# Making less of the last S5 layer in advance: V and the taps move back into the layer, powers, rotation and W stay ahead of it

## The chip, the cores and the metric

The kernel runs on one core of one Trainium2 chip. The metric is the device time of one execution in microseconds (us), and the median of several runs is compared. Engines are named as the profile names them: PE is TensorE (matmuls and transposes), PEld its weight loads, DVE is VectorE, ACT is ScalarE, POOL is GpSimd, and SP is SyncE, which here only issues DMAs. ACT issues a few DMAs too.

## The reference, cut to what matters

The program is a trunk of four layers over 512 tokens of width 1024, in float32. Layer 0 is an S5 mixer, layer 1 an HGRN2 mixer, layer 2 sliding-window attention, and layer 3 an S5 mixer again with its own weights.

```python
for i in range(4):
    u = rms_norm(h, norm_pre[i])
    y = (s5_branch, hgrn2_branch, swa_branch)[i % 3](u, ...)
    h = h + rms_norm(y, norm_post[i])

# s5_branch: 64 groups of 16 channels, 64 complex states each
proj = h @ w_in; u, z = split(proj)
a = exp(lambda * dt)                 # complex, one per group and state
b = (a - 1) / lambda * B             # complex input matrix
x_t = a * x_{t-1} + b @ u_t          # scan over the 512 tokens
y = gelu(2 * Re(C @ x) + d * u)
y = y * sigmoid(y @ w_glu + b_glu)
return (y * silu(z)) @ w_out
```

What an S5 layer needs besides its activations depends on its parameters alone: the powers a^0 to a^8, the input matrix over a chunk of eight tokens (V), the output matrix over a chunk (W), the direct response inside a chunk (the taps, which fill a Toeplitz matrix), and a rotation table for the scan over 64 chunks. None of it depends on the tokens, so it can be made at any time before the layer.

## The kernel before, in words

**Layers.** Every layer begins with the transposed normalised input (`norm_xt`, L279: eight transposes for a 128-token block, each evacuated twice, as a rounded high part `xh` on ACT and a remainder `xl` on DVE). Big projections are done as three matmul terms, high by high, high by low and low by high (`ws_steps`, L220; `as_steps`, L235). Weights come in 512 KB pieces by SP and are split in the same way (`w_conv`, L159: `whi` on ACT, `wlo` on DVE). Every layer ends with `out_proj` (L328), whose matmuls are named `ops` and which adds the result to the residual `h` (L350), a tile of 16 KB a partition, and spills `h` to DRAM (`hd`, L356).

**The S5 layer** (`layer_s5`, L1026). The 64 groups are handled as eight blocks b of eight groups. For a block, `s5_u` (L837) evacuates a projection to `ut`, writes it to DRAM (`ub`) and reads it back with the chunks spread over partitions (`u`). `s5_core` (L854) multiplies V by u (`xps`), rotates, scans (`r`, L879), rotates back into `spre`, and adds two products, Toeplitz by u and W by states (`yps`, L902 and L904). The result goes through gelu and two transposes a pair of blocks to `y`. `s5_rest` (L928) is the input projection itself, 16 blocks of PE work of which the first four are done in halves of 256 tokens. After it `s5_yparts` (L983) splits `y` into `yh` and `yl`, and `s5_glu_first` (L997) begins the gate's projection.

In layer 0 the constants are made inside the layer: `s5_tables` (powers), `s5_v` (V, L747), `s5_taps` (L779: 8 small matmuls `kps`, 8 transposes `tps`, 2 transposes `ktp`, and 8 DMAs that fill the Toeplitz matrix `toep`), `s5_rot` and `s5_w`. In layer 3 `s5_load` (L652) loads all of it from DRAM: V, rotation, taps (as 8 DMAs a block straight into `toep`) and W.

The order inside an S5 layer is written out: each part is a Python generator that yields (engine, cost, marks it needs), and `Flow` (L58) picks again and again the step that can start first by those planned costs. The queues of PE, DVE, ACT and SP follow that order. A DMA is planned with 4.5 us to landing, a block's eight `toep` DMAs with 0.6 us of the DMA queue.

**What is made ahead** (before). `ahead_plan` (L625) makes a list of jobs for layer 3: one `ahead_base` (powers and tables), four `ahead_rot`, and eight `ahead_block` (L557), each of which makes V, the taps and W of one block and writes them to DRAM. A job is a generator too. The HGRN layer calls `ahead(1)` at 88 places (L1299, L1306), the attention layer `ahead(3)` after each of its 22 steps (L1486). Base and rotation take 40 calls, a block takes 12, so HGRN has room for four blocks, and attention makes the other four. The jobs' tiles lie where `h` lies: both layers release `h` first (`close_h`) and load it again from `hd` behind the jobs (`open_h`, L1514).

In these two layers the order is not written out by hand: the framework's scheduler places the instructions by its own estimates. Buffers are handed out in program order, though. The jobs' `kps`, `tps` and `ktp` take PSUM buffers of the tag `ca`, of which there are two, and the HGRN core (`dps`, `sps`, `bps`, `cps`), the attention scores (`scps`, L1364) and the input transposes (`xtp`) take theirs from the same two.

**Attention** (`layer_at`, L1417) runs the steps of `ATSEQ` (L48): c is the softmax of a pair of heads over one 128-token block (`at_core`, L1346), g a gate (`at_gate`), q and z projections. The last steps are c12, z3, c13 and four gates.

Of the kernel before, what the change touches and what calls it, by code (L numbers as in the profile page):

```python
# [108 lines left out]
class Trunk:  # L109
# [447 lines left out]
    def ahead_block(self, j, b):  # L557
        nc, a = self.nc, self.a
        gs = slice(8 * b, 8 * b + 8)
        shp = [P, 8, 8, 16]  # L560
        with self.tc.tile_pool(name="ahead", bufs=1, reuse_waits="tile") as s:
            prm = s.tile([P, 4, 128], F32, tag="prm", name="prm")
            nc.sync.dma_start(out=prm, in_=a["s5_bc"][j, b])
            ap = s.tile([P, 2, 8, 9], F32, tag="ap", name="aps")
            nc.sync.dma_start(out=ap, in_=self.sd["ap"][:, :, gs, :])
            co = s.tile([P, 2, 2, 8], F32, tag="co", name="cos")
            nc.sync.dma_start(out=co, in_=self.sd["co"][:, :, :, gs])
            dm = s.tile([P, 8], F32, tag="dm", name="dms")
            nc.gpsimd.memset(dm, 0.0)
            nc.sync.dma_start(out=dm[0:16, :], in_=a["s5_d"][j][:, gs])  # L570
            c1 = s.tile([P, 8, 32], F32, tag="c1", name="c1")
            nc.gpsimd.memset(c1[:, :, 16:32], 0.0)
            yield
            B = prm.rearrange("p k (g h) -> p k g h", h=16)
            q = s.tile([P, 2, 8, 16], F32, tag="q12", name="q12")
            q2 = s.tile([P, 2, 8, 16], F32, tag="q12b", name="q12b")
            nc.vector.tensor_tensor(out=q, in0=B[:, 0:2], in1=bc(co[:, 0].unsqueeze(3), [P, 2, 8, 16]), op=ALU.mult)
            nc.vector.tensor_tensor(out=q2, in0=B[:, 0:2][:, ::-1], in1=bc(co[:, 1].unsqueeze(3), [P, 2, 8, 16]), op=ALU.mult)
            nc.vector.tensor_tensor(out=q, in0=q, in1=q2, op=ALU.add)
            nc.scalar.activation(out=c1[:, :, 0:16], in_=B[:, 2], func=AF.Copy, scale=self.cst[:, CO_SGN:CO_SGN + 1])  # L580
# [5 lines left out]
            nc.vector.tensor_tensor(out=t2, in0=bc(ap[:, 1, :, 0:8].unsqueeze(3), shp), in1=bc(q[:, 1].unsqueeze(2), shp), op=ALU.mult)
            yield
            nc.vector.tensor_tensor(out=vt, in0=vt, in1=t2, op=ALU.add)
            yield
            vtf = vt.rearrange("p g j h -> p g (j h)")  # L590
            kps = self.psum.tile([P, 2, 128], F32, tag="ca", name="kps", bufs=2)
            for g in range(8):
                c = 32 * (g % 4)
                nc.tensor.matmul(kps[c:c + 32, g // 4, :], lhsT=c1[:, g, :], rhs=vtf[:, g, :], start=True, stop=True)
            kt = s.tile([P, 2, 128], F32, tag="q12b", name="kt")
            nc.scalar.activation(out=kt, in_=kps, func=AF.Copy)
            yield
            v = s.tile([P, 8, 128], F32, tag="v", name="v")
            for hh in range(2):
                tps = self.psum.tile([P, 4, 128], F32, tag="ca", name="tps", bufs=2)  # L600
                for g in range(4):
                    nc.tensor.transpose(tps[:, g, :], vtf[:, 4 * hh + g, :], self.ident)
                nc.scalar.activation(out=v[:, 4 * hh:4 * hh + 4, :], in_=tps, func=AF.Copy)
            nc.sync.dma_start(out=self.sd["v", b], in_=v)
            yield
            ktp = self.psum.tile([P, 2, 4, 32], F32, tag="ca", name="ktp", bufs=2)
            for i in range(2):
# [1079 lines left out]
```

## Time and profile before

Three runs of the kernel before took 1133.0, 1134.98 and 1136.96 us; the median is 1134.98 us. The profiled execution took 1136.95 us, of which 1135.1 us lie between its first and last instruction.

| engine | busy us | share of the span | instructions |
|---|---|---|---|
| PE | 1040.9 | 92% | 6480 |
| PEld | 824.9 | 73% | 6480 |
| DVE | 750.9 | 66% | 1466 |
| ACT | 498.1 | 44% | 921 |
| POOL | 93.7 | 8% | 167 |

The span divides about so: layer 0 to 264 us, HGRN to 586, its output projection to 630, attention to 857, its output projection to 886, the S5 part of layer 3 to 1028, the gate to 1090, and the last output projection to the end. Busy time is what an engine spent in instructions. A busy PE need not be at its peak, since matmuls overlap and run at half speed when the granted clock is at its lower level; the column PEclk gives the granted clock as a share of full speed.

### The profile page before, as it was taken

Reading aid. Unit: us, or ns where it says so; the run is one execution under the profiler, and the core shown is the slowest. Engines: PE = TensorE matmul, PEld = TensorE weight load, DVE = VectorE, ACT = ScalarE, POOL = GpSimd, SP = SyncE. Lnnn points to the kernel's source line nnn. Section 1 sums busy time; section 2 is a strip of 40 time slices with the busy share of each in tenths; the row PEclk is TensorE's granted clock in tenths of the full one; section 3 lists DMA queues with packets and bytes.
Section 4 is the critical chain, followed back from the end, with each engine's and each line's share of the span. In section 5 each row is a group of like instructions: output and inputs, shape, how many; then the busy total and the mean of one; then the engine's idle time right before and its main releaser. Section 6 shows DMA issues by size and latency. Waiting matters only on the chain. (4 is left out here: it accounts for less than half of the span.)

```text
span 1135.1 us, 17074 instructions
## 1 busy us (share of the span) xinstructions
PE 1040.9 (92%) x6480; PEld 824.9 (73%) x6480; DVE 750.9 (66%) x1466; ACT 498.1 (44%) x921; POOL 93.7 (8%) x167
## 2 busy tenths in 40 slices
PE   5999976999899999999999899999979989988997
PEld 4755544778899898988968886666637867766876
DVE  6686759585698877687865755877836435643752
ACT  4344426554442324243234424587544436644441
POOL 2000000120200001000001021100000100000200
PEclk9999987999999999999999899999969989998999
DMA  5564233534242313422263254331512567844231
GB/s 226 145 183 129 61 95 89 178 113 153 96 131 92 101 43 122 126 91 74 90 224 112 84 148 111 108 98 64 180 63 94 172 194 230 246 154 148 93 111 56
DMA packets 77185, 142.69 MB, mean 126 GB/s; under 512 B 33584, under 2 KB 44592, under 8 KB 75952
## 3 DMA queue, kind: packets, MB, share of 16 engines
q1 hardware_dynamic: 72128, 126.32, 35.9%
q10 hardware_dynamic: 4976, 15.28, 4.1%
q8 instruction: 51, 0.84, 0.3%
q14 instruction: 30, 0.25, 0.1%
HBM read 107.53 MB, written 24.87 MB: 117 GB/s over the span
## 5 line engine op out<-in xcount | busy, mean ns | idle before, releaser
L183 DVE TENSOR_TENSOR wlo<-wraw,whi 128x1024 fp32r<-128x1024 f32 x116 | 144.9, 1264 | 102.1 <-ACT whi L182 90.9
L228 PE MATMUL pj<-xh,whi 128*128 128x512 f32 (+1 forms) x496 | 180.6, 367 | 1.5 <-ACT rraw L1337 1.5
L228 PE MATMUL pj<-xl,whi 128*128 128x512 f32 (+1 forms) x496 | 177.7, 360 | 0.0
L228 PE MATMUL pj<-xh,wlo 128*128 128x512 f32 (+1 forms) x496 | 176.8, 357 | 0.0
L182 ACT ACTIVATE whi<-wraw 128x1024 fp32r<-128x1024 f32 x116 | 121.0, 1056 | 81.0 <-PE pj L228 41.2
L228 PE MATMUL pj<-xf,wraw 128*128 128x512 f32 (+1 forms) x320 | 116.7, 514 | 0.0
L228 PEld LDWEIGHTS pj<-xh,whi 128*128 128x128 f32 x496 | 96.4, 196 | 16.8 <-issue 4.3
L228 PEld LDWEIGHTS pj<-xl,whi 128*128 128x128 f32 x496 | 96.4, 195 | 14.5 <-issue 3.6
L243 PE MATMUL ops<-whi,gh 128*128 128x512 f32 x256 | 101.6, 399 | 4.5 <-ACT gh L1089 2.2
L228 PEld LDWEIGHTS pj<-xh,wlo 128*128 128x128 f32 x496 | 96.1, 194 | 12.6 <-issue 1.1
L243 PE MATMUL ops<-wlo,gh 128*128 128x512 f32 x256 | 100.7, 394 | 2.6 <-DVE wlo L183 2.6
L243 PE MATMUL ops<-whi,gl 128*128 128x512 f32 x256 | 100.3, 394 | 0.1
L228 PEld LDWEIGHTS pj<-xf,wraw 128*128 128x128 f32 x320 | 59.8, 194 | 40.5 <-issue 36.7
L243 PEld LDWEIGHTS ops<-whi,gh 128*128 128x128 f32 x256 | 48.0, 188 | 16.4 <-ACT gh L1089 3.0
L243 PEld LDWEIGHTS ops<-wlo,gh 128*128 128x128 f32 x256 | 48.1, 188 | 14.9 <-DVE wlo L183 5.1
L243 PEld LDWEIGHTS ops<-whi,gl 128*128 128x128 f32 x256 | 48.1, 188 | 11.7 <-DVE gl L1090 0.9
L228 PE MATMUL pj<-yl,whi 128*128 128x512 f32 x128 | 51.2, 400 | 2.5 <-DVE yl L994 2.5
L228 PE MATMUL pj<-yh,whi 128*128 128x512 f32 x128 | 51.7, 404 | 2.0 <-ACT whi L182 2.0
L228 PE MATMUL pj<-yh,wlo 128*128 128x512 f32 x128 | 51.2, 400 | 1.1 <-DVE wlo L183 1.1
L243 PE MATMUL vps<-wlo,xh 128*128 128x256 f32 x160 | 45.3, 283 | 0.0
L243 PE MATMUL vps<-whi,xl 128*128 128x256 f32 x160 | 45.3, 283 | 0.0
L243 PE MATMUL vps<-whi,xh 128*128 128x256 f32 x160 | 45.3, 283 | 0.0
(296 smaller groups left out, 2075.3 us busy)
## 6 DMA issues: line engine op xcount, KB each, us to landing
wraw<-in_s_in SPq DMA_DIRECT2D x32, 512.0 KB, 5.8
wraw<-in_hg_in SPq DMA_DIRECT2D x32, 512.0 KB, 3.6
wraw<-in_at_in SPq DMA_DIRECT2D x20, 512.0 KB, 4.5
wraw<-in_s_glu SPq DMA_DIRECT2D x16, 512.0 KB, 4.1
wraw<-in_s_out SPq DMA_DIRECT2D x16, 512.0 KB, 3.5
hd<-h SPq DMA_DIRECT2D x6, 1024.0 KB, 4.1
h<-hd ACTq DMA_DIRECT2D x3, 2048.0 KB, 7.9
prm<-in_s_bc SPq DMA_DIRECT2D x16, 256.0 KB, 3.8
```

What stands on the lines that cost most here:

```text
L182: nc.scalar.activation(out=hi, in_=raw, func=AF.Copy)
L183: nc.vector.tensor_tensor(out=lo, in0=raw, in1=hi.bitcast(F32), op=ALU.subtract)
L228: self.nc.tensor.matmul(ps, lhsT=l[k // 4][:, k % 4, c], rhs=r[:, k, n0:n1], start=k == 0 and n == 0, stop=k == KB - 1 and n == len(terms) ...
L243: self.nc.tensor.matmul(ps, lhsT=l[:, k, c], rhs=r[k // per][:, k % per, :], start=k == 0 and n == 0, stop=k == KB - 1 and n == 2)
```

## The change

HGRN makes the base, the rotation and all eight W (`ahead_w`, 6 calls a job, so 48 calls in place of four blocks' 48). V and the taps of layer 3 are made in layer 3 by the functions that layer 0 uses. Layer 3 loads the powers, the coefficients and `d` at its start, and per block the parameters, the rotation and W. The Toeplitz DMAs read from SBUF instead of DRAM. Attention runs no jobs and keeps `h`. Two more edits belong to it: V's and the parameters' tiles lie in the layer's own pool in layer 3, and the first chunk of the gate's weights is converted when input chunk 6 is done (`early`), no longer at the end of the projection.

```diff
-    def ahead_block(self, j, b):
+    def ahead_w(self, j, b):
...
-            prm = s.tile([P, 4, 128], F32, tag="prm", name="prm")
-            nc.sync.dma_start(out=prm, in_=a["s5_bc"][j, b])
-            ap = s.tile([P, 2, 8, 9], F32, tag="ap", name="aps")
+            prm = s.tile([P, 2, 128], F32, tag="prm", name="prm", bufs=2)
+            nc.sync.dma_start(out=prm, in_=self.a["s5_bc"][j, b][:, 2:4])
+            ap = s.tile([P, 2, 8, 9], F32, tag="ap", name="aps", bufs=2)
             nc.sync.dma_start(out=ap, in_=self.sd["ap"][:, :, gs, :])
...
+            c1 = s.tile([P, 8, 16], F32, tag="c1", name="c1", bufs=2)
+            nc.scalar.activation(out=c1, in_=B[:, 0], func=AF.Copy, scale=self.cst[:, CO_SGN:CO_SGN + 1])
             yield
-            vt = s.tile(shp, F32, tag="vt", name="vt")
...
+            w = s.tile(shp, F32, tag="w", name="w", bufs=2)
+            t2 = s.tile(shp, F32, tag="t2", name="t2w")
+            nc.vector.tensor_tensor(out=w, in0=bc(ap[:, 0, :, 1:9].unsqueeze(3), shp), in1=bc(c1.unsqueeze(2), shp), op=ALU.mult)
             yield
...
-        self.jobs = [self.ahead_base(j)] + [self.ahead_rot(pr) for pr in range(4)] + [self.ahead_block(j, b) for b in range(8)]
+        self.jobs = [self.ahead_base(j)] + [self.ahead_rot(pr) for pr in range(4)] + [self.ahead_w(j, b) for b in range(8)]
...
     def s5_load(self, b, m):
-        yield "D", 0.2, (m["y", b - 3],) if b > 2 else ()
-        d = self.d[b] = dict(sp=self.sp[b % 2])
-        d["v"] = s.tile([P, 8, 128], F32, tag="v", name="v", bufs=3)
-        nc.sync.dma_start(out=d["v"], in_=self.sd["v", b])
-        yield m["v", b]
...
-        yield "D", 0.6, (m["y", b - 2],) if b > 1 else ()
-        d["toep"] = toep = self.tp[b % 2]
-        for jj in range(8):
-            n = (jj + 1) * 16
-            nc.sync.dma_start(out=toep[128 - n:128, jj, :, :], in_=self.sd["k", b][0:n])
-        yield m["toep", b]
-        yield "D", 0.2, (m["y", b - 3],) if b > 2 else ()
-        d["w"] = s.tile([P, 8, 128], F32, tag="w", name="w", bufs=3)
-        nc.sync.dma_start(out=d["w"], in_=self.sd["w", b])
+        yield "D", 0.2, (m["c", b],) + ((m["y", b - 2],) if b > 1 else ())
+        w = self.d[b]["w"] = s.tile([P, 8, 128], F32, tag="w", name="w", bufs=2)
+        nc.sync.dma_start(out=w, in_=self.sd["w", b])
         yield m["w", b]
...
     def s5_open(self, j):
-            m8 = s.tile([P, 64], F32, tag="m8", name="m8", bufs=1)
-            nc.sync.dma_start(out=m8, in_=self.sd["m8"])
-            self.s5t = dict(m8=m8)
+            for n, sh in (("ap", [P, 2, 64, 9]), ("co", [P, 2, 2, 64]), ("m8", [P, 64])):
+                self.s5t[n] = s.tile(sh, F32, tag=n, name=n, bufs=1)
+                nc.sync.dma_start(out=self.s5t[n], in_=self.sd[n])
+            dm = self.s5t["dm"] = s.tile([P, 64], F32, tag="dm", name="dm", bufs=1)
+            nc.gpsimd.memset(dm, 0.0)
+            nc.sync.dma_start(out=dm[0:16, :], in_=self.a["s5_d"][j])
...
     def s5_v(self, j, b, m):
+        if j == 0:
+            prm = self.wpool.tile([P, 2, 4, 128], F32, tag="wlo", name="prm", bufs=4)[:, 0]
+        else:
+            prm = self.scr.tile([P, 4, 128], F32, tag="prm", name="prm", bufs=2)
...
     def s5_glu_first(self, glu, y, i0, early, m):
         for c in range(2):
+            if early and c == 0:
+                yield "A", 2.1, (m["cd", 6],)
+                yield "V", 2.6, ()
+                self.w_conv(i0 + 8)
+                self.w_load(i0 + 9)
+                continue
             yield "V", 2.6, (m["rest"],)
...
     def layer_s5(self, L):
             for b in range(8):
                 flow.add(self.s5_core(b, m), 10 * b + 1)
+                flow.add(self.s5_v(j, b, m), 10 * b + 2)
+                flow.add(self.s5_taps(b, m), 10 * b + 3)
...
     def layer_at(self, L, nxt):
-        later = bool(self.jobs)
-        if later:
-            self.close_h()
...
-                self.ahead(3)
-            if later:
-                self.ahead_stop(True)
-                self.open_h(self.hd)
             self.out_proj(L, nxt, self.h)
```

## Rows read from the trace of the kernel before

**Rows 1.** Busy time by stage. Columns: start and end of the stretch, its length, then busy us (instructions) of PE, PEld, DVE, ACT and POOL, the granted PE clock, the DMA engines' share, and GB/s. In order: HGRN, the start of attention, its middle, its tail, the start of layer 3, its blocks, the crossing to the gate, and, out of order, one block of layer 0 late in that layer.

```profile
264.00:586.00 322.00, 310.62 (x2277) 280.59 (x2277) 245.34 (x572) 114.44 (x202) 21.61 (x52) 0.99 0.32 104
630.00:700.00 70.00, 61.01 (x393) 54.29 (x392) 42.94 (x77) 25.75 (x49) 11.10 (x6) 0.95 0.42 113
700.00:828.00 128.00, 127.94 (x610) 85.67 (x610) 96.51 (x261) 84.24 (x199) 7.20 (x11) 1.00 0.37 120
828.00:857.00 29.00, 19.20 (x54) 8.37 (x52) 10.67 (x42) 13.76 (x37) 0.00 (x0) 0.65 0.02 6
886.00:924.00 38.00, 30.87 (x224) 29.00 (x222) 12.62 (x26) 12.84 (x28) 3.91 (x9) 0.94 0.69 215
924.00:1028.00 104.00, 96.48 (x814) 77.71 (x815) 52.46 (x66) 57.01 (x81) 2.54 (x2) 0.96 0.68 205
1028.00:1042.00 14.00, 8.44 (x20) 5.24 (x20) 9.44 (x12) 8.54 (x13) 0.00 (x0) 0.65 0.53 186
162.00:181.00 19.00, 16.02 (x118) 8.95 (x116) 17.94 (x23) 11.44 (x19) 1.54 (x3) 0.94 0.41 105
```

**Rows 2.** What PE waited for between 264 and 1040 us, longest in total first. Columns: the waiting line and the releaser, us in total, times, longest.

```profile
PE xtp L292 <- DVE xl L298: 10.4, 3, 5.4
...
PE yps L904 <- DMA w<-sd: 5.3, 2, 4.2
```

**Rows 3.** PE in order of time while attention's last job is made and the softmax step c12 begins (start, duration, what).

```profile
811.71 0.64 PE L594 MATMUL kps<-vt,c 128*32 128x128 f32 x16
812.29 0.66 PE L602 MATMUL tps<-cst,vt 128*128 128x128 f32 x4
812.70 0.48 PE L243 MATMUL ops<-wlo,gh 128*128 128x512 f32 x1
...
813.25 0.60 PE L602 MATMUL tps<-cst,vt 128*128 128x128 f32 x4
813.68 0.44 PE L608 MATMUL ktp<-cst,kt 128*128 128x128 f32 x2
813.88 0.47 PE L243 MATMUL ops<-whi,gh 128*128 128x512 f32 x1
...
814.53 1.13 PE L1366 MATMUL scps<-k,q 64*128 64x256 f32 x4
```

**Rows 4.** DVE in order of time before that: the last scores of step c11, then the first operation of that job.

```profile
788.09 0.42 DVE L1373 CUSTOM_DVE_ANT_0 sm<-scps,cst 128x256 f32<-128x256 f32 x1
...
804.69 0.42 DVE L577 TENSOR_TENSOR q<-prm,cos 128x256 f32<-128x256 f32 x1
```

**Rows 5.** DVE at the start of attention, where a job's operations stand between the remainders `xl` of the input.

```profile
636.64 0.42 DVE L577 TENSOR_TENSOR q<-prm,cos 128x256 f32<-128x256 f32 x1 [0.45 <-DMA cos<-sd]
...
638.90 1.21 DVE L584 TENSOR_TENSOR vt<-aps,q 128x1024 f32<-128x1024 f32 x1
```

**Rows 6.** Groups of DVE instructions by line between 162 and 180.5 us, a block of layer 0 (busy us, mean ns of one | idle before it).

```profile
L771 DVE TENSOR_TENSOR vt<-ap,q 128x1024 f32<-128x1024 f32 x1 | 1.2, 1199 | 0.0
L760 DVE TENSOR_TENSOR q<-prm,co 128x256 f32<-128x256 f32 x1 | 0.7, 734 | 0.0
...
L762 DVE TENSOR_TENSOR q<-q,q12b 128x256 f32<-128x256 f32 x1 | 0.4, 439 | 0.1
L812 DVE TENSOR_TENSOR ksb<-ktp,dmx 128x128 f32<-128x128 f32 x1 | 0.3, 292 | 12.4 <-issue 12.4
```

**Rows 7.** All instructions that POOL spends on `q12b` in layer 0 (count, then shortest, median and longest ns, first and last start).

```profile
L761 POOL TENSOR_TENSOR q12b<-prm,co x8: 619/622/632, 18.3 to 180.6; 128x256 f32<-128x256 f32 x8
```

**Rows 8.** ACT in the same block of layer 0: one of the two evacuations of `tps`.

```profile
174.53 0.60 ACT L800 ACTIVATE v<-tps 128x512 f32<-128x512 f32 x1
```

**Rows 9.** SP's DMA issues at the start of layer 3, in order of time; a duration covers the issues of a row with the waits between them.

```profile
886.16 0.33 SPq L695 DMA_DIRECT2D m<-sd  x1
891.29 0.33 SPq L356 DMA_DIRECT2D hd<-h  x1
...
900.12 13.35 SPq L669 DMA_DIRECT2D toep<-sd  x16
...
915.10 0.38 SPq L846 DMA_DIRECT2D ub<-ut  x1
```

**Rows 10.** PE in layer 3: the first `xps` of block 0, with the idle time before it, and its first `yps`.

```profile
924.40 1.98 PE L865 MATMUL xps<-u,v 128*64 128x64 f32 x32 [5.57 <-DMA u<-ub]
...
938.28 0.44 PE L902 MATMUL yps<-toep,u 128*64 128x128 f32 x4
```

**Rows 11.** DVE at the start of layer 3: the first remainder of the third token block.

```profile
895.65 0.35 DVE L298 SCALAR_TENSOR_TENSOR xl<-xtp,gpre,xh 128x128 fp32r<-128x128 f32 x1 [1.51 <-ACT xh L296]
```

**Rows 12.** PE at the crossing from the input projection to the gate, with the idle time before a row and what ended it.

```profile
1030.34 0.50 PE L228 MATMUL pj<-yh,whi 128*128 128x512 f32 x1 [1.44 <-ACT whi L182]
...
1038.68 0.79 PE L228 MATMUL pj<-yh,wlo 128*128 128x512 f32 x1 [1.11 <-DVE wlo L183]
```

**Rows 13.** The page's row on the reload of `h` (count, size, median us from issue to landing).

```profile
h<-hd ACTq DMA_DIRECT2D x3, 2048.0 KB, 7.9
```

**Rows 14.** The reload of `h` behind HGRN, in ACT's queue, and the first use of `h` after it, on DVE, in order of time.

```profile
580.79 0.34 ACTq L1517 DMA_DIRECT2D h<-hd  x1
...
596.46 1.28 DVE L350 SCALAR_TENSOR_TENSOR h<-yg,rs_r,h 128x1024 f32<-128x1024 f32 x1 [0.94 <-POOL rs_r L254]
```

**Rows 15.** The page's row on the loads of the parameters `prm` (count, size, median us from issue to landing).

```profile
prm<-in_s_bc SPq DMA_DIRECT2D x16, 256.0 KB, 3.8
```

More of the change, by code (lines that the diff above doesn't have):

```diff
@@ L576, in ahead_block @@
[L576 to L580, printed above, removed]
+            c1 = s.tile([P, 8, 16], F32, tag="c1", name="c1", bufs=2)
@@ L585, in ahead_block @@
             yield
[L586 to L607, printed above, removed]
-                nc.tensor.transpose(ktp[:, i].rearrange("p g h -> p (g h)"), kt[:, i, :], self.ident)
-            dmx = s.tile([P, 8, 16], F32, tag="dmx", name="dmx")
-            nc.gpsimd.tensor_tensor(out=dmx, in0=bc(dm.unsqueeze(2), [P, 8, 16]), in1=bc(self.cst[:, CO_EYE16:CO_EYE16 + 16].unsqueeze(1), [P, 8, 16]), op=ALU.mult)
@@ L611, in ahead_block @@
-            ksb = s.tile([P, 2, 4, 16], F32, tag="ksb", name="ksb")
-            nc.vector.tensor_tensor(out=ksb, in0=ktp[:, :, :, 0:16], in1=dmx.rearrange("p (a g) h -> p a g h", a=2), op=ALU.add)
-            nc.sync.dma_start(out=self.sd["k", b], in_=ksb.rearrange("p a g h -> p (a g) h"))
-            yield
-            w = s.tile(shp, F32, tag="vt", name="w")
-            t2 = s.tile(shp, F32, tag="t2", name="t2w")
-            nc.vector.tensor_tensor(out=w, in0=bc(ap[:, 0, :, 1:9].unsqueeze(3), shp), in1=bc(c1[:, :, 0:16].unsqueeze(2), shp), op=ALU.mult)
@@ L645, in ahead, with ahead_stop @@
                 self.job = None
-    def ahead_stop(self, last):
-        while self.job is not None or (last and self.jobs):
+    def ahead_stop(self):
+        while self.job is not None or self.jobs:
             self.ahead(1)
@@ L750, in s5_v @@
         gs = slice(8 * b, 8 * b + 8)
-        yield "D", 0.2, (m["w2", b - 2], m["vt", b - 1]) if b > 1 else (m["vt", 0],) if b else ()
-        prm = self.wpool.tile([P, 2, 4, 128], F32, tag="wlo", name="prm", bufs=4)[:, 0]
+        last = "w2" if j == 0 else "v"
+        yield "D", 0.2, (m[last, b - 2], m["vt", b - 1]) if b > 1 else (m["vt", 0],) if b else ()
+        if j == 0:
+            prm = self.wpool.tile([P, 2, 4, 128], F32, tag="wlo", name="prm", bufs=4)[:, 0]
+        else:
+            prm = self.scr.tile([P, 4, 128], F32, tag="prm", name="prm", bufs=2)
         nc.sync.dma_start(out=prm, in_=self.a["s5_bc"][j, b])
         B = prm.rearrange("p k (g h) -> p k g h", h=16)
-        yield "V", 1.3, (m["ap"],) + ((m["kt", b - 1],) if b else ())
+        yield "V", 1.3, (m["ap"],) + ((m["kt", b - 1],) if b and j == 0 else ())
         t = self.s5t
@@ L768, in s5_v @@
         shp = [P, 8, 8, 16]
-        yield "V", 1.2, (m["v", b - 2], m["w2", b - 2]) if b > 1 else ()
-        vt = self.wpool.tile(shp, F32, tag="wlo", name="vt", bufs=4)
+        yield "V", 1.2, (m["v", b - 2], m[last, b - 2]) if b > 1 else ()
+        if j == 0:
+            vt = self.wpool.tile(shp, F32, tag="wlo", name="vt", bufs=4)
+        else:
+            vt = self.scr.tile(shp, F32, tag="vt", name="vt", bufs=2)
         nc.vector.tensor_tensor(out=vt, in0=bc(t["ap"][:, 0, gs, 0:8].unsqueeze(3), shp), in1=bc(q[:, 0].unsqueeze(2), shp), op=ALU.mult)
@@ L790, in s5_taps @@
         yield "A", 0.4, ()
-        kt = self.tab.tile([P, 2, 128], F32, tag="q12b", name="kt", bufs=1)
+        kt = self.tab.tile([P, 2, 128], F32, tag="q12b" if self.kt is None else "kt", name="kt", bufs=1)
         nc.scalar.activation(out=kt, in_=kps, func=AF.Copy)
```

38 lines of the change are left out of this document (13 added, 25 removed).

## The prediction, made before the changed kernel was run

> **What bounds the kernel now.** I read the stages first [rows 1]: for each stretch how long PE was busy, at what granted clock, and how busy the others were. In HGRN PE is busy 310.62 of 322 us at clock 0.99, in the middle of attention 127.94 of 128 us at 1.00, while DVE is at 76% and 75%. A stretch like that gets shorter when work leaves PE's queue and longer when some comes in. Three stretches are different. The start of attention has 9 us without PE, its tail 29.00 - 19.20 = 9.8 us, at a clock of 0.65, and layer 3 has 38.00 - 30.87 + 104.00 - 96.48 = 14.65 us, with DMA at 0.69 and 0.68 and DVE at about half. The second view, PE's waits, says who ended the idle times [rows 2]: the remainders `xl` on DVE at the starts of layers (5.4 us of it in attention), and in layer 3 the DMA of W (5.3 us); the first `xps` waited 5.57 us for `u` [rows 10]. The order of instructions around those places then shows why, and that is taken up part by part.
>
> **The sum's base.** Durations are from the profiled execution: 1136.95 us, 1.85 us more than its span of 1135.1, and 1.97 us above the median of the runs, 1134.98. I sum against 1136.95 and take off 1.97 at the end.
>
> **The price of V and the taps of one block on PE.** From the first `kps` to the first other matmul 812.70 - 811.71 = 0.99 us pass, from the second `tps` to the next other matmul 813.88 - 813.25 = 0.63 us [rows 3]; 1.62 us in all. The four durations together give 0.64 + 0.66 + 0.60 + 0.44 = 2.34 us, but they overlap with their neighbours. I take 1.62, bounds 1.6 to 2.3: four blocks are 6.5 us (to 9.4), eight are 13.0 us (to 18.7).
>
> **HGRN.** It loses four blocks' V and taps and gains four W jobs. PE loses 6.5 us. On DVE a whole block was 3 x 0.42 + 6 x 1.22 + 0.29 = 8.87 us by the same shapes [rows 5, 6], four are 35.5; eight W at 3 x 1.22 = 3.66 us are 29.3, so DVE loses 6 us too. ACT loses four times `c1`, `kt` and two `v`, each at most 0.60 us [rows 8]. Of the DMAs 4 x (4 loads + 3 stores) = 28 become 8 x 3 = 24, in the same places of the program. The calls come out even (40 + 48 = 88), so nothing is left for the end: the last W still leaves before `h` is fetched. That fetch was issued at 580.79, takes 7.9 us, and `h` is used at 596.46 [rows 13, 14], so 596.46 - 580.79 - 7.9 = 7.8 us cover a later last job; beyond that each us costs one. I take -6.0, a little under PE's share; bounds -9.4 and +2 (a job's wait of a few us that the scheduler puts before the HGRN core on DVE).
>
> **Attention, removed matmuls.** Four blocks again, in stretches where PE is full: -6.5, bounds 0 to -9.4.
>
> **Attention, start.** While PE waits for `xl`, DVE runs the job's `q`, its second product, the addition and `vt` between the remainders: 636.64 to 638.90 + 1.21, of which 3 x 0.42 + 1.2 = 2.4 us are the job's [rows 5]. They stand ahead of the transposes that end PE's 5.4 us wait. What is late next is the rest of the chain, the rope table in front of it on DVE, which stays. -2.4, bounds 0 and -5.4.
>
> **Attention, tail.** c12's first scores start at 814.53, right behind the job's `ktp` at 813.68 [rows 3]. c11's last scores were read at 788.09, so their PSUM buffer had long been free; but the eighth job's `kps`, `tps` and `ktp` come before c12 in the program and take the tag's two buffers first, and that job only began on DVE at 804.69 [rows 4]. So c12 and c13 ran late, and after 828 us they had PE to themselves, with too little else to fill it. Without jobs c12 can start up to some 20 us sooner, beside the output projection's matmuls that now run before it. At full clock the 19.20 us of PE in the tail would be about 19.20 x 0.65 = 12.5, so 29 - 12.5 = 16.5 us are there to be had. The scheduler will order this anew by its own estimates, and c13 keeps a last softmax chain of its own: I take half, -8; bounds 0 and -16.
>
> **Attention, h.** Closing and reloading `h` goes. The reload's 2 MB were covered by the tail; nothing. The spill to DRAM still runs, as before.
>
> **Layer 3, blocks.** Added per block: PE 1.62; DVE 0.73 + 0.44 + 3 x 1.22 + 0.29 = 5.1 us [rows 6]; ACT at most 4 x 0.60 = 2.4 [rows 8]; POOL 0.62 [rows 7]. DVE then has 12.62 + 52.46 + 41 = 106 of 142 us, ACT at most 89, PE 30.87 + 96.48 + 13.0 = 140.4 [rows 1]. So PE decides: with all 14.65 us of idle time filled the stage would be 142 - 1.6, with none filled 142 + 13. Two things fill. The Toeplitz DMAs of the first two blocks hold SP for 13.35 us, so that block 0's `ub` is issued only at 915.10 and `u` keeps PE waiting 5.57 us [rows 9, 10]; in the changed order block 0's taps are ready only after its projection, so `ub` goes ahead of them. And V's 512 KB a block become 256 KB of parameters, the taps no longer come from DRAM: the 5.3 us for W [rows 2] should shrink. SP's count of issues stays at 12 a block. I take 10 of the 14.65 as filled: +3.0.
>
> **Layer 3, start.** New waits: the first `q` on DVE waits for the table loads and `prm`. The tables can go where `m8` went, at 886.16. If `prm` goes behind the spill of `h` at 891.29 [rows 9], it lands 3.8 us later [rows 15], at 895.1 or after, and `q` and `vt` (2.4 us), planned ahead of the third token block, run at the moment when `xl` used to start, 895.65 [rows 11]. Behind them in DVE's queue wait the `xl` of both late token blocks, and PE's second halves wait for these. 0 if `prm` overtakes the spill, 2.4 + 2.4 (the rest of V between the two sets) if not: I take +3.0, since `v` stood behind that spill too.
>
> **Layer 3, crossing.** Converting the first gate chunk early takes its 2 x 1.2 us off DVE and as much off ACT where PE waits 1.44 and 1.11 us at a clock of 0.65 [rows 1, 12]. The second chunk's conversion slides forward into its place, so `yl` still waits: -2.5, bounds 0 and -5. Its price is a weight load that may hold SP while input chunk 6 is still on PE; behind it stand only the last blocks' loads.
>
> **Sum.** -6.0 - 6.5 - 2.4 - 8 + 3.0 + 3.0 - 2.5 = -19.4. 1136.95 - 19.4 - 1.97 = 1115.6, say 1116 us.
>
> **Two rules of the Trainium skill.** In layer 0 `q` takes 0.73 us beside POOL's `q12b` of 0.62 us [rows 6, 7], in the jobs, without POOL, 0.42 [rows 5]: the layer's way costs DVE 0.31 us a block more on this product. The Trainium skill (SBUF — State Buffer, section "SBUF: two separate sides") says that DVE and GpSimd share a port pair as an exclusive lock, and that the loser is blocked for the whole instruction. By that rule DVE would lose 0.62 us a block and 5 us in all, by the rows 2.5; DVE has 36 us to spare in the stage, so the sum stays as it is by either.
>
> The other one speaks against the whole reading. The Trainium skill (Perfetto Trace Analysis, section "Identifying the Most-Contended Engine") says that matmul busy time does not measure how near PE is to its limit, because matmuls overlap, and that the share of weight loads does. It is the rule behind rival 2; the rows agree in so far as PEld is at 280.59 of 322 in HGRN, but at 85.67 of 128 in the middle of attention [rows 1].
>
> **The rivals.**
> 1. *The tail stays.* The scheduler fills PE with the output projection before c12 as it does now, and the tail starves as before. For it: order comes from estimates, and a lighter program changes these everywhere. Against it: the PSUM order that held c12 is gone. 1115.6 + 8 = 1124.
> 2. *PE's busy time is no limit in HGRN and attention.* If the small matmuls ran in the shadow of chains on DVE and ACT, then taking them out gives nothing: 1115.6 + 6.0 + 6.5 = 1128. For it: DVE at 75%. Against it: PE's longest waits [rows 2] lie at the starts of layers and in layer 3, not in these stretches.
> 3. *Everything fills.* All of the tail's 16 us and all idle time of layer 3, without a late start: 1115.6 - 8 - 4.6 - 3 = 1100.
> 4. *Slower: layer 3 becomes a chain as late in layer 0.* There a block takes 19 us with DVE busy 17.94 [rows 1], because scan, V, conversion and the taps of the next block follow each other in one queue. With 19 us a block from the first `xps` at 924.4 on, and 938.28 - 924.40 = 13.9 us for a block's own way [rows 10], the last `yps` comes at 924.4 + 7 x 19 + 13.9 = 1071, while PE's own work in this sum ends at 1028 + 6 = 1034. That is 37 us more: 1153. For it: the same code ran so. Against it: W (3.66 us) and the rotation are not made here, which alone gives 15.3 us a block. It decides from 7p + 938.3 = 1034 + 19.4 on, which is p = 16.5 us a block.
>
> **How the numbers follow.** Forecast 0.44 (own range 1108 to 1123), rival 1 0.20, rival 2 0.12, rival 3 0.12, rival 4 0.12, of which a third ends near or below the old time. The range leaves out the deep end of rival 3 and most of rival 4: 1101 to 1132. Within 0.3% (3.4 us, about what a measurement of this kernel can tell from no change) lies the milder part of rival 4 and the upper edge of rival 2: 0.06. Slower 0.10, faster 0.84.
>
> **What would show it.** Right: HGRN from its first to its last matmul about 6 us shorter; attention's DVE with nothing but its own work between the `xl`; c12's scores within some 10 us of c11's last; a tail with a clock well above 0.65; in layer 3 `ub` of block 0 ahead of the first `toep`, PE's waits for `u` and W under 3 us, and blocks 13 to 15 us apart. Wrong: `kps` waiting for `vt`, or `yps` for `toep`, by several us each in layer 3; `xl` of layer 3 behind a `q` that waits for `prm` for over 5 us; a tail of attention as long and as slow as before; HGRN as long as before.

## The result and the profile after

The changed kernel took 1117.31 us (median of 4 runs, 1115.33 to 1119.54), the kernel before beside it 1135.97 (4 runs, 1133.0 to 1137.18). The ratio is 0.984, with a 95% interval of 0.9811 to 0.9869. The forecast was 1116, so the total came out within 1.3 us of it. The terms did not: four are far off, and that their errors cancel is luck.

The profiled execution of after took 1116.3 us with a span of 1114.5. The page's first part:

```profile
PE 1031.2 (93%) x6480; PEld 822.3 (74%) x6480; DVE 750.5 (67%) x1458; ACT 504.2 (45%) x933; POOL 103.2 (9%) x162
```

The engines did nearly the same work as before. To see where time went, I cut each trace at the last `ops` matmul of every layer's output projection. The first two lengths hold a layer with its output projection, the third the last layer up to the start of its last matmul, and the fourth is the way from that layer's start to its first `yps`. The runs of the experiments stand in the table too.

| kernel | HGRN | attention | last layer | first `yps` | median us |
|---|---|---|---|---|---|
| before | 330.0 | 263.5 | 241.6 | 52.1 | 1135.97 |
| after | 316.1 | 235.3 | 264.0 | 67.6 | 1117.31 |
| e1, lean | 315.3 | 234.8 | 238.8 | 49.6 | 1091.73 |
| e2, no jobs in attention | 331.4 | 235.2 | 243.1 | 50.6 | 1108.9 |
| e3, jobs sooner | 330.0 | 256.1 | 242.6 | 52.2 | 1129.63 |
| e4, `prm` sooner | 317.6 | 233.2 | 263.3 | 61.0 | 1115.59 |
| e5, V later | 316.5 | 235.0 | 262.7 | 52.3 | 1116.28 |
| e6, both | 317.7 | 237.1 | 266.5 | 53.2 | 1122.91 |
| e7, nothing waits | 317.6 | 236.8 | 264.4 | 65.8 | 1114.82 |
| e8, no PE part | 314.9 | 235.1 | 256.9 | 55.2 | 1112.43 |
| e9, not early | 317.5 | 237.1 | 272.7 | 65.6 | 1120.89 |
| e10, one block ahead | 323.6 | 237.2 | 242.5 | 45.0 | 1104.7 |
| e11, no DVE part | 318.8 | 237.1 | 251.1 | 52.2 | 1104.6 |
| e12, two blocks ahead | 322.1 | 239.2 | 246.9 | 53.2 | 1109.41 |

The lengths are of one profiled execution each, and those lie off their medians by up to 8 us (e9's at 1128.6 us above it, e8's at 1107.9 below), so the medians decide where the two differ. The HGRN of kernels in which that layer is the same (after, e4 to e9, e11) differs by up to 4 us, so smaller differences say little. After minus before: -13.9, -28.2, +22.4, and -1.0 in layer 0: -20.7 together, as the spans (1135.1 - 1114.5 = 20.6).

The next rows are windows of the two traces, with the columns of [rows 1]. Before: HGRN until 10 us ahead of its last `zps`, the rest of HGRN with its output projection, the start of attention, the rest of attention, the last layer until the gate's first matmul.

```profile
292.30:556.00 263.70, 253.81 (x1925) 233.74 (x1924) 206.37 (x505) 88.47 (x152) 15.20 (x38) 0.99 0.31 99
556.00:622.30 66.30, 64.09 (x383) 51.89 (x382) 44.26 (x72) 29.90 (x56) 6.45 (x15) 1.00 0.44 151
622.30:655.50 33.20, 27.76 (x210) 27.51 (x209) 22.72 (x44) 13.38 (x29) 2.42 (x8) 0.90 0.28 80
655.50:885.80 230.30, 216.90 (x1042) 152.10 (x1041) 151.33 (x372) 128.16 (x289) 21.24 (x24) 0.96 0.34 106
...
886.10:1030.30 144.20, 128.15 (x1041) 107.01 (x1039) 64.98 (x91) 71.44 (x111) 6.45 (x11) 0.95 0.69 210
```

After, the same five, then two slices of 12 us at the start of the last layer:

```profile
291.20:547.40 256.20, 249.90 (x1887) 231.15 (x1885) 208.10 (x501) 86.08 (x150) 13.61 (x27) 0.99 0.33 106
547.40:607.30 59.90, 59.24 (x325) 48.77 (x320) 37.74 (x60) 27.16 (x50) 6.94 (x14) 1.00 0.41 150
607.30:637.60 30.30, 26.91 (x210) 26.43 (x209) 17.62 (x37) 14.27 (x29) 1.72 (x5) 0.94 0.30 93
637.60:842.70 205.10, 202.23 (x938) 145.14 (x937) 121.83 (x339) 125.84 (x278) 20.04 (x15) 0.99 0.27 82
...
843.00:1011.50 168.50, 145.62 (x1249) 119.52 (x1247) 106.23 (x141) 85.00 (x144) 18.26 (x28) 0.94 0.57 169
855.00:867.00 12.00, 4.40 (x26) 3.50 (x24) 7.28 (x13) 3.37 (x10) 1.51 (x2) 0.73 0.84 246
867.00:879.00 12.00, 11.38 (x80) 10.60 (x81) 5.04 (x14) 5.16 (x13) 0.00 (x0) 0.70 0.21 50
```

In the rest of attention PE's idle time fell from 13.4 to 2.9 us: the starved tail of [rows 1] is gone. In the last layer the opposite happened: PE was idle for 16.05 us of the stretch before and for 22.9 after, and two slices near its start ran at a clock of 0.73 and 0.70, in one of which PE was busy for 4.40 of 12 us.

### The profile page after: what moved, and what is told of

The parts are those of the page before. It is cut to its first block, busy times and chain, and to the rows that moved or that the text cites. A ratio compares the mean times of both kernels' runs of the same rounds, so it can differ in the third digit from the quotient of the medians.

```text
span 1114.5 us, 17031 instructions
## 1 busy us (share of the span) xinstructions
PE 1031.2 (93%) x6480; PEld 822.3 (74%) x6480; DVE 750.5 (67%) x1458; ACT 504.2 (45%) x933; POOL 103.2 (9%) x162
## 4 chain that ended last, share of the span: by engine, by line
PE 63%; DVE 15%; ACT 6%; DMA 6%; issue 5%; SPq 2%; POOL 1%; ACTq 1%; DVEq 0%; POOLq 0%
PE pj L228 26%; PE ops L243 13%; PE zps L243 4%; PE vps L243 3%; PE sps L1120 2%; PE scps L1328 2%; DVE wlo L183 2%; SPq L773 2%; ACT whi L182 2%; PE aops L1364 2%; DMA rsw<-rraw 1%; DMA prm<-in_s_bc 1%; PE ptp L1359 1%; DVE sg L1049 1%; PE yps L858 1%
## 5 line engine op out<-in xcount | busy, mean ns | idle before, releaser
L341 DVE TENSOR_TENSOR yg<-ops,gpost 128x512 f32<-128x512 f32 x32 | 21.9, 688 | 36.9 <-ACT junk L339 36.6
```

The source lines that it names most:

```text
L341: nc.vector.tensor_tensor(out=yg[:, tb, f], in0=ps, in1=gp[:, f], op=ALU.mult)
```

## The experiments

**Which layer gave what (e1 to e3).** e1 is the first three layers of after with the last layer of before; V and the taps are not made at all, and W is loaded in their place:

```diff
-        self.jobs = ... + [self.ahead_block(j, b) for b in range(8)]
+        self.jobs = ... + [self.ahead_w(j, b) for b in range(8)]
+            w = self.sd["w", b] = self.sd["v", b] = dr([P, 8, 128], F32, ...)
+            self.sd["k", b] = w[:, 0, :].rearrange("p (g h) -> p g h", h=16)
```

> The first three layers of the kernel after with the last layer of the kernel before: only W jobs in HGRN, no jobs in attention, h stays on chip, and the last layer loads V, W and taps from DRAM as before. Left out: V and the taps of the last layer are not computed (W is loaded in their place, in the same sizes). By the terms of the prediction this is -6.0 -6.5 -2.4 -8 = -22.9 us, so about 1113 us. By the stage marks of the two traces (HGRN and its output projection -13.9, attention -28.1) it is -42, so about 1094 us; then the last layer gave 24 us back and not 6.

1091.73 us, ratio 0.9619 (0.9602 to 0.9637), which is 42.4 us under the kernel before beside it (1134.14). So the marks are right: the first three layers gave about twice the 22.9 us of the forecast, and the last layer took some 25 back (1117.31 - 1091.73).

e2 is the kernel before without attention's four blocks:

```diff
-        self.jobs = ... + [self.ahead_block(j, b) for b in range(8)]
+        self.jobs = ... + [self.ahead_block(j, b) for b in range(4)]
```

> The kernel before with HGRN as it was (four whole blocks) and attention without its four blocks; h stays on chip in attention; the last layer loads the first four blocks twice. Left out: V, W and taps of blocks 4 to 7. By the prediction's terms for attention -6.5 -2.4 -8 = -16.9, about 1119 us. By the stage marks -28, about 1108 us. The difference to the run with only W jobs in HGRN is HGRN's own part: 6 us by the prediction, 14 by the marks.

1108.9 us, ratio 0.9768 (0.975 to 0.9785): -25.2 for attention alone. The 17.2 us from e2 to e1 are HGRN's and what little the last layers differ by (HGRN alone, 331.4 to 315.3, is 16).

e3 leaves all the work of the kernel before and moves it forward:

```diff
-                self.ahead(3)
+                self.ahead(5)
```

> The kernel before with one number changed: five calls of the jobs at each step of attention instead of three, so that the last job's kps, tps and ktp come in PE's order ahead of c12 and of the output projection. Nothing is left out. Theory (the tail starved because the last job's place in the order of PE and of the scores' PSUM buffers held c12 and c13): the tail comes back nearly whole with all the jobs still in attention, -10 to -16 us, 1120 to 1126 us; PE's clock in attention's last 60 us stays at 1.00. Rival (the tail starved because DVE's whole load in attention was too high, and only taking the jobs out mends it): under 4 us, 1132 us or more. A second rival: the jobs crowd the middle and what is won in the tail is lost there, within 3 us of before.

1129.63 us, ratio 0.9959 (0.9941 to 0.9977): -4.5, between the two. Windows of e3: the start of attention, its middle, and what was the tail:

```profile
622.50:656.00 33.50, 27.64 (x212) 27.43 (x211) 22.69 (x44) 13.39 (x29) 2.22 (x7) 0.90 0.30 82
656.00:830.00 174.00, 167.17 (x854) 119.86 (x854) 122.86 (x320) 105.08 (x234) 18.18 (x14) 0.99 0.41 124
830.00:850.00 20.00, 15.47 (x55) 8.03 (x55) 7.83 (x26) 10.98 (x30) 0.00 (x0) 0.83 0.00 1
```

That is none of the three forecasts. The tail is more than half mended: 4.5 us idle and 2.6 lost to a clock of 0.83, against 9.8 idle and 6.7 lost at 0.65 in [rows 1]. But the middle, which was idle for 3.6 us before (655.5 to 828), is now idle for 6.8, attention is 7.4 us shorter, and 4.5 are left of it in the median. So the order that I blamed, the last job's PSUM buffers ahead of c12, is a part of the tail; the rest goes only when the jobs go (e2).

**Why the last layer grew (e4 to e8, e11).** The waits of DVE in after's last layer, 843 to 1011.5 us, begin so:

```profile
DVE q L713 <- DMA prm<-in_s_bc: 19.6, 6, 10.8
DVE xl L298 <- ACT xh L296: 5.8, 13, 0.5
```

The obvious suspect is the first row. e4 issues each load of the parameters as soon as its buffer is free and keeps the plan's times:

```diff
-        yield "D", 0.2, (m[last, b - 2], m["vt", b - 1]) if b > 1 else ...
+        yield "D", 0.2, (m["c", b - 2],) if b > 1 else ()
```

> The kernel after with the same order on PE, DVE and ACT, but the load of the parameters of block b issued as soon as the buffer is free (after c1 of block b-2 in the plan) instead of after vt of block b-1. Theory (q waits for prm for 19.6 us in all, 10.8 of it at block 2, and the converted weights, xa and the scan stand behind it): DVE's wait for prm falls from 19.6 to under 8 us and the time by 5 to 12 us, to 1105 to 1112 us. Rival (DVE has slack there; PE's idle time comes from the chain u, xps, xa, scan, yps itself): the waits go and the time stays within 2 us of 1117.

1115.59 us, ratio 0.9801 (0.9776 to 0.9827), against 0.9811 to 0.9869 of after. The wait went from 19.6 to 3.5 us and the first `yps` came 6.6 us sooner, but the last `yps` came only 0.7 us sooner, and the layer took 263.3 us for 264.0. The same view of e4:

```profile
DVE wlo L183 <- ACT whi L182: 17.9, 5, 7.4
...
DVE q L716 <- DMA prm<-in_s_bc: 3.5, 1, 3.5
```

DVE now waits for `whi` instead. The longest wait of DVE, which had time to spare, was worth nothing by the layer's end.

e5 moves the first V behind all four sets of `xl`:

```diff
-                m["ap"].t = 4.5
+                m["ap"].t = 12.0
```

> The kernel after with the plan's time for the table loads set from 4.5 to 12, so that the first q and vt stand behind all four xl sets on DVE. Theory (q waits for prm behind the spill of h, and the xl of both late token blocks wait behind q): PE's waits for xl at the start fall from 6.4 us to under 2, PE no longer runs at half clock there, the first xps comes some 6 us sooner after the last matmul of attention's output projection (44.8 us in the kernel after, 38.7 before): -4 to -8 us, 1109 to 1113 us. Rival (the start is limited by u, whose DMA stands behind the eight Toeplitz DMAs on SP): within 2 us of 1117.

1116.28 us, ratio 0.9823 (0.9792 to 0.9853). The theory's sign was there (first `xps` 34.5 us after the layer's start for 44.4, first `yps` 52.3 for 67.6), yet nothing was left of it at the end: the last `yps` came at 169 us, before the edit at 158. PE's waits in e5's last layer begin so:

```profile
PE yps L858 <- DMA toep<-ksb: 15.3, 5, 3.9
PE kps L745 <- ACT z L936: 3.8, 1, 3.8
PE xtp L292 <- DVE xl L298: 2.0, 1, 2.0
```

The wait for `xl` fell to 2.0 us, as in the kernel before, and a wait for the Toeplitz DMAs took its place. (The rival's number came out, but not by its cause: `u` was issued ahead of the Toeplitz DMAs here.) In the plan `vt` of a block stands behind `vt` of the block before, so a late first V makes all eight late; that this is why was read from the code and not shown by a run.

> Both edits together. If the two causes are separate the gains add: -9 to -20, 1097 to 1108 us, and the last layer up to the gate is near the 150 us that PE's busy time and the old stage make of it. If one chain carries both, the gain is that of the larger one.

1122.91 us, ratio 0.9862 (0.9836 to 0.9888): the two edits together are no better than either, and by these medians some 6 us worse. Neither theory covers that.

e7 lets nothing in the layer wait for V and the taps; they are made, and not used:

```diff
-  lhsT=d["v"][:, g, o:o + 64]
+  lhsT=self.ident[:, o:o + 64]
-  rhs=d["toep"][:, :, g, :]
+  rhs=self.ident
```

> The kernel after in which nothing of the last layer waits for V and the taps: all their instructions and DMAs stay, in the same order on every engine, but xps and the first half of yps multiply by the identity instead of v and toep. Left out: the use of V and the taps in the last layer. Theory A (the 25 us that the last layer grew by are waits: chains from prm over vt, kps, v and the Toeplitz DMAs into PE's queue): the last layer's stretch falls from 168 to about 150 us, the time to 1098 to 1103 us. Theory B (they are the work itself and its places in the queues of PE, DVE and ACT): within 5 us of 1117.

1114.82 us, ratio 0.9814 (0.9785 to 0.9844), the layer at 264.4. So it is not that `xps` and `yps` wait for V and the taps. The run doesn't take away every wait of theory A: in it `kps` still waits for `vt` (6.1 us in PE's queue), and `u` is still issued behind the Toeplitz DMAs, which wait for `ksb`.

e8 leaves PE's and ACT's part of V and the taps out, e11 DVE's and POOL's:

```diff
 e8
-            nc.tensor.matmul(kps..., lhsT=d["c1"][:, g, :], rhs=vtf[:, g, :])
...
-                nc.tensor.transpose(tps[:, g, :], vtf[:, 4 * hh + g, :], self.ident)
+            d["v"] = vtf
 e11
-        nc.vector.tensor_tensor(out=q, ...)
...
-        nc.vector.tensor_tensor(out=vt, in0=vt, in1=t2, op=ALU.add)
+            d["vt"] = bc(self.ident.unsqueeze(1), [P, 8, 128])
```

> The kernel after without kps, tps, ktp on PE and kt and v on ACT in the last layer; xps reads vt and the taps' DMAs read a part of vt, so that DVE's V, the parameters' loads and the Toeplitz DMAs stay, in the same plan. Left out: the transposes of V and the taps' matmuls. PE's busy time in the stretch falls from 146 us to about 128. If PE's work is what the layer costs (Theory B, and the price of a block is 2.2 us instead of the 1.62 of the prediction): -13 to -18 us, 1099 to 1104 us. If the time is in waits for DVE and DMAs (Theory A): under 6 us.

> The kernel after without DVE's and POOL's part of V in the last layer (q, q12b, the addition, vt, t and its addition); kps and the transposes read the identity instead. PE's and ACT's part, the taps' DMAs, the loads and the plan's times stay, except that the first q's place in front of xl is gone. Left out: the computation of V's products. The runs before left PE's part out (stage from 168.5 to 162) and took the waits for V and taps away (168.7): neither is what the layer costs. Theory C (the layer goes by DVE's queue: scan, conversions and V of the next block stand one behind the other, 39 us of V among 106 busy us, and the first q stands in front of xl): the stretch falls to 145 to 152 us, the time to 1095 to 1102 us. Theory D (it is the plan's order, whatever work stands in it): within 6 us of 1117.

e8: 1112.43 us, ratio 0.978 (0.9751 to 0.9808). e11: 1104.6 us, ratio 0.972 (0.9683 to 0.9758). The last layer up to the gate, in e8 and in e11:

```profile
841.70:1004.00 162.30, 133.93 (x1041) 112.42 (x1039) 105.72 (x141) 73.63 (x120) 18.09 (x29) 0.91 0.60 175
```

```profile
846.90:1003.50 156.60, 141.97 (x1250) 117.56 (x1248) 69.19 (x101) 84.62 (x144) 9.95 (x20) 0.96 0.63 183
```

Busy time times clock tells PE's work from the slow clock: 121.7 us before, 136.9 after, 121.9 in e8, 136.3 in e11. V and the taps are 15.1 us of PE's work, 1.9 a block. But e8, without them, is only 5 us under after in the median, which is theory A's number, and PE idles for 28.4 us in it: PE's work alone is not what the layer goes by. e11 has all of PE's work and is 12.7 us under after, between the ranges of theories C and D. By the marks its gain lies at the start: the first `yps` came 15.4 us sooner, while from the first to the last `yps` 93.9 us passed, for 90.5 in after. But e5 has its first `yps` just as soon (52.3 us for 52.2), with V in DVE's queue, and kept nothing of it. So V's work on DVE is worth 12.7 us in this layer, and theory C named the right engine; how much of it falls on the start and how much on the later blocks these runs don't divide. From the first `yps` to the gate 92.1 us pass before the change, 100.9 in after, 107.1 in e8 and 104.4 in e11: neither run gives those 8.8 us back.

**The start given back (e10, e12).** e10 makes block 0 ahead in HGRN, as the kernel before did, and the other seven in the layer; e12 does so with blocks 0 and 1:

```diff
-  [self.ahead_w(j, b) for b in range(8)]
+  [self.ahead_block(j, b) if b < 1 else self.ahead_w(j, b) for b in range(8)]
...
+                if j and b < 1:
+                    flow.add(self.s5_load_v(b, m), 10 * b + 2)
...
-        yield "D", 0.2, (m[last, b - 2], m["vt", b - 1]) if b > 1 else (m["vt", 0],) if b else ()
+        yield "D", 0.2, (m["u", 0],) if j and b == 1 else (m[last, b - 2], m["vt", b - 1]) if b > 1 else ...
```

The last lines are an edit of their own: the first block that is still made in the layer loads its parameters only after block 0's `u`. The two were not tried apart.

> The kernel after with block 0 alone made ahead in HGRN as before the change (V, taps and W stored to DRAM and loaded), the other seven made in the layer. In the kernel after the first yps begins 67.6 us after attention's output projection, in the kernel before 52.1; this run should start as before, which is worth up to 15 us, and HGRN takes back a quarter of its 15 us, some 4. If the start is the layer's loss and stays won: -6 to -11, 1106 to 1111 us. If the later blocks only take the time again (as with V behind xl, where the first yps came at 52.3 and the last not sooner): within 3 us of 1117, or above it by the 4 us of HGRN.

1104.7 us, ratio 0.9728 (0.9704 to 0.9751): faster than both kernels, by some 12.6 us than after, and a little more than foretold. The layer takes 242.5 us, 0.9 more than before the change, with seven blocks of V in it; HGRN takes back 7.5, for 4 in the forecast. The stretch up to the gate:

```profile
852.40:1003.80 151.40, 138.04 (x1214) 114.33 (x1213) 104.57 (x139) 82.18 (x140) 15.65 (x24) 0.98 0.63 181
```

Against after, 9.5 us of idle time are gone (22.9 to 13.4), and of 7.6 us of busy time some 6 are the clock (0.94 to 0.98) and 1.6 block 0's own work.

> The kernel after with blocks 0 and 1 made ahead in HGRN, the other six in the layer. With one block ahead the time was 1104.7, since the layer starts as before. If only the start mattered, the second block costs HGRN's 4 us and gives back at most the 2 to 3 us a block that the layer pays: 1104 to 1108 us. If each block in the layer costs more than it did in HGRN: below 1103 us.

1109.41 us, ratio 0.9765 (0.9738 to 0.9793). That is above both forecasts. The second block brings nothing and by the medians costs 4.7, though the intervals touch: with it `toep` of two blocks stands on SP ahead of `ub` again, as in [rows 9], and the first `xps` comes at 38.9 us for 34.2.

**The crossing (e9).**

```diff
-            flow.add(self.s5_glu_first(glu, (yh, yl), i0, j > 0, m), 110)
+            flow.add(self.s5_glu_first(glu, (yh, yl), i0, False, m), 110)
```

> The kernel after with both conversions of the gate's weights behind the last input chunk, as before the change. Prediction: +2.5 us (1120). Rival (yl waits behind a conversion in either, as the trace of after shows with 3.5 us): within 1.5 us.

1120.89 us, ratio 0.9868 (0.9837 to 0.9899), 0.9811 to 0.9869 with the edit in. The 3.6 us between the medians agree with the forecast's 2.5, but the intervals overlap, so it is not shown.

## Why the prediction was right, and where it was not

**HGRN, -6.0: too small, -13.9.** PE's busy time in the two windows fell by 8.8 us (253.81 + 64.09 - 249.90 - 59.24), the price of the matmuls. The other 5.1 are idle time, 12.1 us before and 7.0 after, of which the forecast had nothing; PE's waits for `gl`, which DVE makes, went from 5.3 to 2.3 us. At the layer's end, for which the forecast said that nothing is left, DVE of the kernel before made the fourth block between the last heads' operations:

```profile
562.00 0.42 DVE L1184 TENSOR_TENSOR hqt<-hqt,hF 128x256 f32<-128x256 f32 x1
562.34 0.41 DVE L577 TENSOR_TENSOR q<-prm,cos 128x256 f32<-128x256 f32 x1
...
563.59 1.23 DVE L584 TENSOR_TENSOR vt<-aps,q 128x1024 f32<-128x1024 f32 x1
...
574.24 1.22 DVE L621 TENSOR_TENSOR w<-w,t2w 128x1024 f32<-128x1024 f32 x1
```

The calls came out even, but where the last block fell was not read. That DVE's part of the blocks made PE idle is read from the order and not shown by a run.

**The price of V on PE, 1.62 us a block: a little low.** It was 2.2 in HGRN (8.8 over four), 2.0 in attention (8.0 over four, below) and 1.9 in the last layer, inside the bounds: between the distance to the next matmul, 1.62, and the sum of the durations, 2.34. Why is not shown.

**Attention, start, -2.4: right** (33.2 to 30.3). **Matmuls, -6.5: right** within the price: PE's busy time in the rest fell by 14.7, of which 6.7 are the tail's slow clock (19.20 - 12.5, [rows 1]) and 8.0 work. **Tail, -8: half of it.** 10.5 us of idle time and 6.7 of slow clock went, 17.2 in all, against the -16 of the far bound. I took half because c13 would keep a softmax chain of its own; in after it has matmuls beside it. PE while c13 ends:

```profile
796.51 1.13 PE L1328 MATMUL scps<-k,q 64*128 64x256 f32 x4
797.57 0.50 PE L243 MATMUL ops<-whi,gl 128*128 128x512 f32 x1
...
806.75 2.69 PE L1364 MATMUL aops<-pt,av 128*64 128x512 f32 x8
809.37 0.50 PE L243 MATMUL ops<-wlo,gh 128*128 128x512 f32 x1
```

The output projection fills the chain and runs on behind it to 843 us. Rival 1 is refuted. So is rival 2's number: e1 gave HGRN's and attention's part in full. That it was PE's part of the blocks that counted there, and not DVE's, rests on PE being busy for nearly all of these windows; no run took the one without the other.

**Layer 3, start, +3.0: this step failed.** The first `yps` came 15.5 us later than before, five times the term. The forecast had the first part of it, with too small a size, and no term for the second. DVE in after:

```profile
852.28 0.89 DVE L277 TENSOR_SCALAR xs<-h,rs_r 128x1024 f32<-128x1024 f32 x1 [2.12 <-POOL rs_r L254]
856.53 0.43 DVE L713 TENSOR_TENSOR q<-prm,co 128x256 f32<-128x256 f32 x1 [3.37 <-DMA prm<-in_s_bc]
857.47 0.42 DVE L715 TENSOR_TENSOR q<-q,q12b 128x256 f32<-128x256 f32 x1 [0.51 <-POOL q12b L714]
857.92 1.22 DVE L727 TENSOR_TENSOR vt<-ap,q 128x1024 f32<-128x1024 f32 x1
859.07 0.34 DVE L298 SCALAR_TENSOR_TENSOR xl<-xtp,gpre,xh 128x128 fp32r<-128x128 f32 x1
...
864.30 1.22 DVE L730 TENSOR_TENSOR t<-ap,q 128x1024 f32<-128x1024 f32 x1
865.55 1.67 DVE L731 TENSOR_TENSOR vt<-vt,t 128x1024 f32<-128x1024 f32 x1
...
872.10 0.35 DVE L298 SCALAR_TENSOR_TENSOR xl<-xtp,gpre,xh 128x128 fp32r<-128x128 f32 x1 [0.43 <-ACT xh L296]
```

And in e10, without V there:

```profile
861.62 0.89 DVE L277 TENSOR_SCALAR xs<-h,rs_r 128x1024 f32<-128x1024 f32 x1 [2.12 <-POOL rs_r L254]
863.44 0.35 DVE L298 SCALAR_TENSOR_TENSOR xl<-xtp,gpre,xh 128x128 fp32r<-128x128 f32 x1 [0.94 <-ACT xh L296]
...
873.65 0.35 DVE L298 SCALAR_TENSOR_TENSOR xl<-xtp,gpre,xh 128x128 fp32r<-128x128 f32 x1 [0.43 <-ACT xh L296]
```

From `xs` to the last `xl` 19.8 us pass in after and 12.0 in e10: 7.8 us, the q, its wait and V as listed, where I had 4.8 as the upper bound, because I let `prm` land just as the first `xl` would begin and so put q's wait, 3.37 us, at nothing. Nor did I see that `xs` itself would start later (last section). I then stopped at DVE. PE, starved here, had its clock granted at the lower level for a good part of 855 to 879 us (0.73 and 0.70 on the mean, above); and after that `u` was issued after the eight Toeplitz DMAs of the same block, which wait for `ksb`:

```profile
850.18 0.34 SPq L356 DMA_DIRECT2D hd<-h  x1
850.62 0.38 SPq L706 DMA_DIRECT2D prm<-in_s_bc  x1
...
875.66 0.38 SPq L802 DMA_DIRECT2D ub<-ut  x1
876.09 0.57 SPq L617 DMA_DIRECT2D w<-sd  x1
879.14 5.04 SPq L773 DMA_DIRECT2D toep<-ksb  x8
884.23 0.59 SPq L806 DMA_DIRECT2D u<-ub  x1
```

`ub` went ahead of `toep`, as foretold; `u` did not, and left 8.6 us behind its `ub`, for 4.5 in e10, where `toep` is ahead of both. All this makes 6.2 of the 15.5 us: the first `xps` came 44.4 us after the layer's start, for 38.3 before. The other 9.3 lie between the first `xps` and the first `yps`, 23.2 us for 13.9 [rows 10]. There block 2's `q` stands in DVE's queue ahead of block 0's `xa` and waits for its parameters, while the `xps` that `xa` reads are long done. DVE, and PE's `xps`:

```profile
894.61 0.42 DVE L713 TENSOR_TENSOR q<-prm,co 128x256 f32<-128x256 f32 x1 [10.79 <-DMA prm<-in_s_bc]
...
898.16 0.68 DVE L830 TENSOR_TENSOR xa<-xps,rotf 128x512 f32<-128x512 f32 x1
```

```profile
887.46 1.15 PE L821 MATMUL xps<-u,v 128*64 128x64 f32 x32 [0.73 <-DMA u<-ub]
```

e4 took that wait away and had its first `yps` 6.6 us sooner, but its last one only 0.7. So what a late first `yps` costs in the end is not this difference alone. The direct measure is e10: without block 0's V the layer is 21.5 us shorter (264.0 - 242.5), block 0's work in it. That is more than the start's loss, since e10 starts 7.1 us sooner than the kernel before too (45.0 us for 52.1), with eight Toeplitz DMAs ahead of `ub` in place of sixteen.

**Layer 3, blocks, +3.0: too small, +8.8.** So much longer is the way from the first `yps` to the gate (92.1 to 100.9 us). The two waits that were to fill did go: PE's for `u` from 5.6 to 0.7 us, and its 5.3 for W altogether. But others came, 5.3 for `vt` and 2.5 for `v` among them, and in place of "10 of 14.65 filled" PE's idle time up to the gate rose by 6.8 (16.05 to 22.9). e10 holds seven blocks for +0.9 us in the whole layer, but that is two errors against each other: up to the gate it is 7.2 us longer than before (144.2 to 151.4), with 2.7 us less idle time (16.05 to 13.4), and its gate is 6.4 us shorter (97.4 to 91.0 from its first matmul to the last of the layer), since it doesn't wait for `yl` (2.5 us before, 3.5 in after) and runs at clock 1.00 (0.95 before). Rival 4, the chain of layer 0, did not come: 90.5 us from the first to the last `yps` in after are 12.9 a block, under the 16.5 at which it decides.

**Crossing, -2.5: agrees** (97.4 to 95.5 for the gate), not shown.

**The sum.** HGRN and attention gave 19.2 us more than forecast and the last layer took 18.9 more: 15.5 + 8.8 - 1.9 = +22.4 for +3.5. The total is right by luck. e10, with one block back in HGRN, comes to 1104.7, near rival 3's 1100.

## What to carry to other kernels

A stage that has idle engines can still have no room at its start: read where the first instances of moved work fall in the queue, and sum what every engine behind that place loses, not only the one that is delayed. Try giving the first instance to the stage before and leaving the others (12.6 us here), and try it before the waits, since the longest wait in a list can be worth nothing. Follow a gain to the stage's end: in e4 and e5 a first result that came sooner was lost again by the last. A total that comes out right says little for its terms: cut both traces at the same marks first.

## What was not expected of the hardware

The forecast had DVE's `q` at 0.73 us beside POOL's `q12b` at 0.62 [rows 6, 7]. In the last layer it was the other way round. POOL in after, beside the `q` of 0.43 us at 856.53 above:

```profile
856.54 0.89 POOL L714 TENSOR_TENSOR q12b<-prm,co 128x256 f32<-128x256 f32 x1 [3.93 <-DMA prm<-in_s_bc]
```

POOL's product was longer here by 0.27 us, and DVE was not slowed, but its addition waited 0.51 us. Which of the two was longer went by which began first. In seven pairs of layer 0 before the change, `q` began 0.11 to 0.18 us after `q12b` and took 0.72 to 0.79 us beside POOL's 0.62; in six pairs of after's last layer it began 0.01 to 0.11 us ahead and took 0.42 to 0.43 us beside 0.79 to 0.89. The Trainium skill (SBUF — State Buffer, section "SBUF: two separate sides") has the two engines share a port pair as an exclusive lock, which goes to the operation that starts first; these rows agree as to who pays.

One more such meeting is in no term of the forecast. DVE's first `xs` of the last layer, while POOL clears `toep`, before and after:

```profile
885.98 0.75 DVE L277 TENSOR_SCALAR xs<-h,rs_r 128x1024 f32<-128x1024 f32 x1 [1.73 <-POOL rs_r L254]
```

```profile
842.87 2.62 DVE L277 TENSOR_SCALAR xs<-h,rs_r 128x1024 f32<-128x1024 f32 x1 [1.73 <-POOL rs_r L254]
```

POOL's first clearing took 1.40 us before and 0.95 after: the engine that was held up changed. The 1.9 us stand in the chain to the first `xps`: the next `xs` begins 9.4 us after this one, for 7.4 before. All runs with after's last layer have them but e11, whose `xs` took 0.75 us again; so a part of e11's earlier start is this and not V.

The other thing is how little PE's work counted where PE was idle for 14%: e8 took 15 us of it away for 5 us of time. In attention, where PEld is busy for 152.10 of 230.30 us, and in HGRN the matmuls' term came out in full or more (with DVE's and ACT's part gone too). The Trainium skill (Perfetto Trace Analysis, section "Identifying the Most-Contended Engine") names the share of weight loads, beside the matmuls' FLOPs, as the measure of that; here PE's idle time told the two stages apart, and PEld's share (107.01 of 144.20 in the last layer before) did not.
